# Splitting every weight tile by halves, with 32 bytes of space behind the rings

## The chip, the cores and the metric

One core of a Trainium2 chip runs the whole program in one launch. The metric is the time of that launch on the device in microseconds (us), the median of several runs. TensorE, VectorE (DVE), ScalarE (ACT), GpSimd (POOL) and SyncE (SP) each work through a list of instructions of their own in order and meet at semaphores.

## The reference

A trunk of two layers works on 256 tokens of width 1024, in f32. Each layer is a token mixer followed by product-key expert retrieval; the changed code feeds the weights to both.

```
for l in range(2):
    h = rms_norm(x) * (1 + sc1) + sh1
    x = x + g1 * mixer(h @ w_in) @ w_out
    h = rms_norm(x) * (1 + sc2) + sh2
    x = x + g2 * peer_ffn(h)

def peer_ffn(h):
    q = h @ wq
    sc = q . keys                       # 8 heads x 2 halves x 128 keys
    top 16 of each half, then top 16 of the 256 sums -> 16 experts a head, softmax gate
    act = gelu(h . u_tab[expert])
    return sum(gate * act * v_tab[expert])
```

## The kernel before

The experts are not gathered. The kernel computes all 16384 of them: 128 columns of the table `u` (128 experts each) give activations, which are multiplied by gates that are zero for the experts not chosen, and 128 rows of `v` bring the result back. So each layer streams 300 weight tiles of 128 x 1024 f32 (512 KB) from memory: 20 of `w_in`, 8 of `w_out`, 16 of `wq`, 128 of `u` (the stage "up", two halves of 64), 128 of `v` (the stage "down").

TensorE multiplies in a rounded f32 format, so each tile is split into `hi` (the rounded value) and `lo` (the rest), and each product is three matmuls: hi x hi, hi x lo, lo x hi (L361 to L363 for an up column, 24 matmuls of 256 columns; L927 for a down row, 12 of 512). The class `Stream` does this. `load` brings a tile into one of 4 `raw` buffers (SP issues the DMA). `split_halves` makes `hi` and `lo` in rings of 3 tiles. So the split of tile n needs the ring's place that tile n-3 leaves, and the load of tile n+4 the `raw` buffer that tile n leaves. There are three ways to make `lo`, and `kind` deals the tiles out to them by the shares in the table `SHARE` (by layer and stage: first half of up, second half, first half of down, second half) and `MIXSHARE`:

- "dve": ScalarE copies `raw` to `hi` (L201), VectorE subtracts, `lo = raw - hi` (L203);
- "pool": the same with the subtraction on POOL (L203 too);
- "dma": ScalarE writes `lo = -raw` rounded (L196), a DMA issued by POOL adds `raw` to it in memory (L197), ScalarE writes `hi` (L198).

A "dma" tile is split in two halves of 512 columns, k = 0 and 1; the others are split as a whole. `ahead`, called after each product, splits as far as `AHEAD = 2` tiles past the one now used (and a first half more, if that tile is "dma").

Beside the weights runs background work, fed in by `Background`: generators that emit a few VectorE instructions at a time with a charge in us, as long as the charged VectorE time is no more than 2 us ahead of the modelled TensorE time (2.6 us a column). `LOCOST` is what a "dve" `lo` is charged. In the first half of up it is the top-16 search (L787 to L838) and, in layer 0, modulation vectors (L285); in the second half and in down it is the gates (L865 to L886). The build's scheduler then orders each engine's list by when operands are expected and by program order.

Of the kernel before, what the change touches and what calls it, by code (L numbers as in the profile page):

```python
# [10 lines left out]
F32 = mybir.dt.float32  # L11
# [7 lines left out]
P = 128  # L19
D = 1024  # L20
# [16 lines left out]
MIXSTEP = 3.4  # L37
RANKS = (3, 2, 4, 1)
MODCOST = 1.2
LOCOST = 1.1  # L40
HALF = D // 2
MIXSHARE = {"dma": 0.4}
CONVCOST = 0.45
# [3 lines left out]
KTAKE = 3  # L47
CONVRANK = 2.5
PACE = (1.0, 2.6)
SHARE = (({"pool": 0.8}, {"dma": 0.25}, {"dma": 0.2}, {}),  # L50
         ({"pool": 0.7, "dma": 0.3}, {"dma": 0.25}, {"dma": 0.2}, {"dma": 0.1}))
NCOL = 94
NROW = 64 + 256 + 256 + 128
# [7 lines left out]
class Carve:  # L61


    def __init__(self, *tiles):
        self.tiles = tiles
        self.reset()
# [77 lines left out]
class Stream:  # L144
# [10 lines left out]
    def __init__(self, nc, pool, aps, bg):  # L155
        self.nc, self.pool, self.aps, self.bg = nc, pool, aps, bg
        self.nd = self.ns = 0
        self.raw = {}
        self.hi, self.lo = [pool.tile([P, self.RING, D], F32R, name=name) for name in ("hi", "lo")]
        self.depth = self.RAW  # L160
        self.share = {}
        self.acc = {"dma": 0.0, "pool": 0.0}
        self.by, self.kinds = "dve", {}
# [20 lines left out]
    def split_halves(self, upto):  # L184

        nc = self.nc
        while self.ns <= min(upto, 2 * len(self.aps) - 1):
            n, k = divmod(self.ns, 2)
            by = self.kind(n)
            if by != "dma" and upto < 2 * n + 1:  # L190
                return
            self.load(n)
            cols = slice(HALF * k, HALF * k + HALF) if by == "dma" else slice(0, D)
            raw, hi, lo = self.raw[n][:, cols], self.hi[:, n % self.RING, cols], self.lo[:, n % self.RING, cols]
            if by == "dma":
                nc.scalar.activation(out=lo, in_=raw, func=AF.Copy, scale=-1.0)  # L196
                nc.gpsimd.dma_start(out=lo, in_=raw, accum_op=ALU.add)  # L197
                nc.scalar.activation(out=hi, in_=raw, func=AF.Copy)  # L198
                self.ns += 1
            else:  # L200
                nc.scalar.activation(out=hi, in_=raw, func=AF.Copy)  # L201
                eng = nc.gpsimd if by == "pool" else nc.vector
                eng.tensor_tensor(out=lo, in0=raw, in1=hi.bitcast(F32), op=ALU.subtract)  # L203
                if by == "dve":
                    self.bg.charge(LOCOST)
                self.ns += 2
            if self.ns % 2 == 0:
                del self.raw[n]
                self.load(n + self.depth)
# [9 lines left out]
class Trunk:  # L219
# [35 lines left out]
        return self.stream.get(n)  # L255

    def ahead(self):
        self.stream.split_halves(2 * (self.pos + self.stream.AHEAD))

    def col(self, l, off, n):  # L260
        return self.cols[:, l * NCOL + off:l * NCOL + off + n]
# [676 lines left out]
    def experts(self, l, area):  # L938
# [13 lines left out]
        acts = [self.big(32, T) for _ in range(2)]  # L952
        self.stream.share = SHARE[l][0]
        run = self.up(hb, acts)
        next(run)
        self.stream.share = SHARE[l][1]
        acts += [self.big(32, T) for _ in range(2)]
# [5 lines left out]
        for i in range(2):  # L963
            self.bg.add(self.gates(1, acts[2:4], i, kept))
        self.stream.share = SHARE[l][2]
        run = self.down(acts)
        next(run)
        self.stream.share = SHARE[l][3]
        self.m = Carve(self.big(), self.big())
# [213 lines left out]
```

## Time and profile before

| what | value |
|---|---|
| median of 3 runs | 2092.47 us (2085.89 to 2093.71) |
| the profiled execution, its own time | 2067.38 us |
| its span, first to last instruction | 2065.3 us |
| TensorE busy | 1909.7 us, 92% of the span |
| mean granted TensorE clock | 0.968 |

A row of the profile's page or of the trace names a line of the kernel (L203), an engine, what is written and read (`lo<-raw,hi`), how often, and times. PE is TensorE and PEld its loading of weights. "Idle before" is time in which the engine did nothing ahead of the instruction, with what released it. The profiled execution is one run; its time is 1.2% under the median.

### The profile page before, as it was taken

The numbers are of one execution on the slowest core, as the hardware profiler recorded it, in microseconds if no ns is written. First come the engines' busy times: TensorE is split into PE (matmuls) and PEld (weight loads), VectorE is DVE, ScalarE is ACT, GpSimd is POOL, SyncE is SP. The second block draws the span as 40 slices with busy tenths as digits, with TensorE's granted clock in tenths as the row PEclk, the third lists the DMA queues.
The fourth block names the chain that finished last, engine by engine and source line by source line (L and its number), as shares of the span: only waits on it lengthen the run. The fifth ranks groups of instructions, "written<-read, shape, count | busy, mean of one in ns | idle before, by whom it ended". The sixth has DMA issues, their size and how long they took to land.

```text
span 2065.3 us, 36257 instructions
## 1 busy us (share of the span) xinstructions
PE 1909.7 (92%) x13718; PEld 1703.1 (82%) x13718; DVE 1417.3 (69%) x2949; ACT 1085.2 (53%) x1790; POOL 472.3 (23%) x361
## 2 busy tenths in 40 slices
PE   6897887999999999899998999888999999999998
PEld 4786887999999776678887899888999987777776
DVE  7887799467765877687568679904467668755554
ACT  4665533544455544545567665555554555555554
POOL 0112355651111111100011225766311111110001
PEclk7888998999999999999999999999999999999999
DMA  8987745757778888887657678777878888876673
GB/s 288 282 256 221 219 166 182 253 189 230 245 245 242 261 271 298 277 321 251 188 160 193 181 194 216 202 208 223 233 246 248 250 244 263 240 209 211 204 205 111
DMA packets 156945, 471.32 MB, mean 228 GB/s; under 512 B 17724, under 2 KB 19041, under 8 KB 156514
## 3 DMA queue, kind: packets, MB, share of 16 engines
q1 hardware_dynamic: 122786, 407.13, 57.6%
q0 software_dynamic: 33984, 61.88, 17.0%
q8 instruction: 107, 1.75, 0.3%
q14 instruction: 68, 0.56, 0.1%
HBM read 388.72 MB, written 18.36 MB: 197 GB/s over the span
## 4 chain that ended last, share of the span: by engine, by line
PE 49%; DMA 25%; DVE 12%; issue 7%; ACT 4%; POOL 2%; SPq 0%; POOLq 0%; DVEq 0%; ACTq 0%
PE acc L927 24%; DMA lo<-raw 17%; PE bank L363 7%; PE bank L361 7%; PE bank L362 7%; DMA raw<-v 3%; DMA raw<-u 2%; DVE lo L203 2%; DVE big L285 2%; DMA big<-wmod 1%; ACT hi L201 1%; POOL lo L197 1%; PE bank L878 1%; PE acc L878 1%; DVE big L817 1%
## 5 line engine op out<-in xcount | busy, mean ns | idle before, releaser
L363 PE MATMUL bank<-mid,lo 128*128 128x256 f32 x2432 | 699.5, 288 | 69.1 <-DMA lo<-raw 43.6
L201 ACT ACTIVATE hi<-raw 128x1024 fp32r<-128x1024 f32 x482 | 512.0, 1062 | 451.5 <-issue 193.3
L361 PE MATMUL bank<-mid,hi 128*128 128x256 f32 x2432 | 700.6, 289 | 5.5 <-ACT mid L1066 5.0
L362 PE MATMUL bank<-mid,hi 128*128 128x256 f32 x2432 | 692.9, 285 | 1.1 <-DVE mid L1069 1.1
L203 DVE TENSOR_TENSOR lo<-raw,hi 128x1024 fp32r<-128x1024 f32 x387 | 479.9, 1240 | 222.2 <-ACT hi L201 220.1
L927 PE MATMUL acc<-hi,mid 128*128 128x512 f32 x2048 | 579.1, 400 | 0.7 <-ACT mid L912 0.6
L363 PEld LDWEIGHTS bank<-mid,lo 128*128 128x128 f32 x2432 | 468.1, 193 | 82.1 <-DMA lo<-raw 54.9
L197 POOL DMA_DIRECT2D lo<-raw x236 | 204.7, 870 | 1204.9 <-ACT lo L196 894.4
L361 PEld LDWEIGHTS bank<-mid,hi 128*128 128x128 f32 x2432 | 467.7, 193 | 9.8 <-ACT mid L1066 7.4
L362 PEld LDWEIGHTS bank<-mid,hi 128*128 128x128 f32 x2432 | 468.1, 193 | 3.3 <-DVE mid L1069 2.6
L927 PEld LDWEIGHTS acc<-hi,mid 128*128 128x128 f32 x2048 | 383.6, 189 | 90.1 <-ACT mid L912 1.0
L927 PE MATMUL acc<-lo,mid 128*128 128x512 f32 x1024 | 330.2, 400 | 22.8 <-DMA lo<-raw 22.6
L203 POOL TENSOR_TENSOR lo<-raw,hi 128x1024 fp32r<-128x1024 f32 x95 | 243.3, 2567 | 124.5 <-ACT hi L201 124.5
L912 ACT ACTIVATE mid<-big 128x256 fp32r<-128x256 f32 x256 | 106.3, 416 | 304.3 <-PE acc L927 298.7
L927 PEld LDWEIGHTS acc<-lo,mid 128*128 128x128 f32 x1024 | 193.4, 189 | 79.2 <-DMA lo<-raw 32.8
L913 DVE TENSOR_TENSOR mid<-big,mid 128x256 fp32r<-128x256 f32 x256 | 108.1, 424 | 145.1 <-PE acc L927 105.5
L198 ACT ACTIVATE hi<-raw 128x512 fp32r<-128x512 f32 x236 | 147.6, 626 | 92.1 <-PE bank L362 42.9
L196 ACT ACTIVATE lo<-raw 128x512 fp32r<-128x512 f32 x236 | 147.0, 623 | 45.0 <-PE acc L927 43.6
L285 DVE SCALAR_TENSOR_TENSOR big<-big 128x1025 f32<-128x1025 f32 x96 | 129.1, 1352 | 42.9 <-DMA big<-wmod 42.5
L886 DVE SCALAR_TENSOR_TENSOR big<-acc,big 128x256 f32<-128x256 f32 x128 | 49.2, 418 | 80.3 <-PE acc L878 80.3
L873 DVE TENSOR_TENSOR og<-o,gidx 128x512 f16<-128x512 f16 x256 | 100.7, 434 | 1.1 <-PE bank L878 0.6
L897 ACT ACTIVATE big<-bank 128x256 f32<-128x256 f32 x256 | 93.6, 366 | 0.0
(200 smaller groups left out, 1583.1 us busy)
## 6 DMA issues: line engine op xcount, KB each, us to landing
raw<-u SPq DMA_DIRECT2D x256, 512.0 KB, 4.7
raw<-v SPq DMA_DIRECT2D x256, 512.0 KB, 4.1
lo<-raw POOLq DMA_DIRECT2D x236, 256.0 KB, 5.6
big<-wmod SPq DMA_DIRECT2D x96, 512.5 KB, 5.9
raw<-win SPq DMA_DIRECT2D x40, 512.0 KB, 5.3
raw<-wq SPq DMA_DIRECT2D x32, 512.0 KB, 4.6
kept<-o SPq DMA_DIRECT2D x64, 256.0 KB, 5.7
o<-kept SPq DMA_DIRECT2D x64, 256.0 KB, 4.6
```

The lines of the kernel that those rows point to most:

```text
L196: nc.scalar.activation(out=lo, in_=raw, func=AF.Copy, scale=-1.0)
L197: nc.gpsimd.dma_start(out=lo, in_=raw, accum_op=ALU.add)
L198: nc.scalar.activation(out=hi, in_=raw, func=AF.Copy)
L201: nc.scalar.activation(out=hi, in_=raw, func=AF.Copy)
L203: eng.tensor_tensor(out=lo, in0=raw, in1=hi.bitcast(F32), op=ALU.subtract)
L285: nc.vector.scalar_tensor_tensor(out=w, in0=w, scalar=1.0, in1=sc, op0=ALU.mult, op1=ALU.mult, accum_out=self.modT[:, l, j:j + 1])
L361: mm(out, whi, hhi, start=start, stop=False)
L362: mm(out, whi, hlo, start=False, stop=False)
L363: mm(out, wlo, hhi, start=False, stop=stop)
L912: nc.scalar.activation(out=a[:, 0], in_=src, func=AF.Copy)
L913: nc.vector.tensor_tensor(out=a[:, 1], in0=src, in1=a[:, 0].bitcast(F32), op=ALU.subtract)
L927: nc.tensor.matmul(self.acc[2 * tt + d], a[:, s, P * tt:P * tt + P], w[:, 512 * d:512 * d + 512], start=i == 0 and s == 0 and w is whi, st ...
```

## The change

`split_halves` treats every tile as it treated the "dma" tiles: in two halves of 512 columns, so that ScalarE, VectorE and POOL get two instructions of half the width. `ahead` asks for two whole tiles past the present one. `LOCOST` is now charged per half, and the "pool" share of layer 0's first half of up is 0.6. An unused tile `pad` of 8 f32 words lies behind the two rings, so all later tiles start 32 bytes higher.

```
@@ -37,7 +37,7 @@
 MIXSTEP = 3.4
 RANKS = (3, 2, 4, 1)
 MODCOST = 1.2
-LOCOST = 1.1
+LOCOST = 0.6
 HALF = D // 2
 MIXSHARE = {"dma": 0.4}
 CONVCOST = 0.45
@@ -47,7 +47,7 @@
 KTAKE = 3
 CONVRANK = 2.5
 PACE = (1.0, 2.6)
-SHARE = (({"pool": 0.8}, {"dma": 0.25}, {"dma": 0.2}, {}),
+SHARE = (({"pool": 0.6}, {"dma": 0.25}, {"dma": 0.2}, {}),
          ({"pool": 0.7, "dma": 0.3}, {"dma": 0.25}, {"dma": 0.2}, {"dma": 0.1}))
 NCOL = 94
 NROW = 64 + 256 + 256 + 128
@@ -157,6 +157,7 @@
         self.nd = self.ns = 0
         self.raw = {}
         self.hi, self.lo = [pool.tile([P, self.RING, D], F32R, name=name) for name in ("hi", "lo")]
+        pool.tile([P, 8], F32, name="pad")
         self.depth = self.RAW
         self.share = {}
         self.acc = {"dma": 0.0, "pool": 0.0}
@@ -187,23 +188,20 @@
         while self.ns <= min(upto, 2 * len(self.aps) - 1):
             n, k = divmod(self.ns, 2)
             by = self.kind(n)
-            if by != "dma" and upto < 2 * n + 1:
-                return
             self.load(n)
-            cols = slice(HALF * k, HALF * k + HALF) if by == "dma" else slice(0, D)
+            cols = slice(HALF * k, HALF * k + HALF)
             raw, hi, lo = self.raw[n][:, cols], self.hi[:, n % self.RING, cols], self.lo[:, n % self.RING, cols]
             if by == "dma":
                 nc.scalar.activation(out=lo, in_=raw, func=AF.Copy, scale=-1.0)
                 nc.gpsimd.dma_start(out=lo, in_=raw, accum_op=ALU.add)
                 nc.scalar.activation(out=hi, in_=raw, func=AF.Copy)
-                self.ns += 1
             else:
                 nc.scalar.activation(out=hi, in_=raw, func=AF.Copy)
                 eng = nc.gpsimd if by == "pool" else nc.vector
                 eng.tensor_tensor(out=lo, in0=raw, in1=hi.bitcast(F32), op=ALU.subtract)
                 if by == "dve":
                     self.bg.charge(LOCOST)
-                self.ns += 2
+            self.ns += 1
             if self.ns % 2 == 0:
                 del self.raw[n]
                 self.load(n + self.depth)
@@ -255,7 +253,7 @@
         return self.stream.get(n)
 
     def ahead(self):
-        self.stream.split_halves(2 * (self.pos + self.stream.AHEAD))
+        self.stream.split_halves(2 * (self.pos + self.stream.AHEAD) - 1)
 
     def col(self, l, off, n):
         return self.cols[:, l * NCOL + off:l * NCOL + off + n]
```

Two places show how the instructions move. The first is ScalarE's list in the second half of up in layer 0, around one "dma" tile and the "dve" tile behind it. L897 is the gelu that empties a column's PSUM bank (L895 after the change, where all lines from `split_halves` on stand two lower). Before:

```order
L198 ACTIVATE hi<-raw 128x512
L196 ACTIVATE lo<-raw 128x512
L198 ACTIVATE hi<-raw 128x512
L897 ACTIVATE big<-bank 128x256
L196 ACTIVATE lo<-raw 128x512
L201 ACTIVATE hi<-raw 128x1024
```

After:

```order
L197 ACTIVATE hi<-raw 128x512
L195 ACTIVATE lo<-raw 128x512
L197 ACTIVATE hi<-raw 128x512
L895 ACTIVATE big<-bank 128x256
L195 ACTIVATE lo<-raw 128x512
L199 ACTIVATE hi<-raw 128x512 x2
```

The "dma" tile's five rows stand as they stood, and the "dve" tile's one `hi` of 1024 columns has become two of 512.

The second place is VectorE's list in the first half of up in layer 0, where the top-16 search (L785 to L798) stands around the `lo` of a "dve" tile. Before:

```order
L787 MAX big<-big 128x8
L203 TENSOR_TENSOR lo<-raw,hi 128x1024
L791 MAX_INDEX big<-big 128x8
L788 MAX_INDEX big<-big 128x8
L798 TENSOR_TENSOR big<-big 128x256
```

After:

```order
L201 TENSOR_TENSOR lo<-raw,hi 128x512
L787 MATCH_REPLACE big<-big 128x256
L785 MAX big<-big 128x8
L788 MAX big<-big 128x8
L201 TENSOR_TENSOR lo<-raw,hi 128x512
L789 MAX_INDEX big<-big 128x8
```

The one `lo` has become two, and three instructions of the search now stand between them.

## Rows read from the trace of the kernel before

**Rows 1.** Windows: stretch, length, busy us (instructions) by engine, PEclk, DMA share, GB/s

```profile
255.00:275.00 20.00, 20.00 (x171) 20.00 (x170) 20.00 (x89) 9.40 (x15) 13.31 (x6) 1.00 0.58 184
...
335.00:355.00 20.00, 17.51 (x133) 17.09 (x132) 20.00 (x14) 7.36 (x11) 14.93 (x5) 0.91 0.72 256
...
375.00:395.00 20.00, 20.00 (x171) 20.00 (x170) 8.70 (x13) 12.13 (x17) 15.69 (x7) 1.00 0.75 246
```

The engines in it are PE, PEld, DVE, ACT, POOL, in this order.

**Rows 2.** Waits of TensorE, whole run: waiting line <- releaser: us, times, longest

```profile
PE bank L363 <- DMA lo<-raw: 43.6, 37, 2.8
PE bank L363 <- DVE lo L203: 24.7, 8, 7.3
PE acc L927 <- DMA lo<-raw: 22.6, 21, 3.1
```

**Rows 3.** Waits of TensorE from 235 to 453 us

```profile
PE bank L363 <- DVE lo L203: 23.2, 6, 7.3
PE bank L363 <- DMA lo<-raw: 1.7, 1, 1.7
```

**Rows 4.** Windows: the first half of up in layer 0

```profile
235.00:453.00 218.00, 193.03 (x1552) 191.37 (x1551) 174.11 (x397) 90.53 (x135) 133.24 (x52) 0.95 0.60 201
```

**Rows 5.** Windows: around the longest wait of that stage

```profile
312.00:319.00 7.00, 0.15 (x2) 0.00 (x0) 7.00 (x5) 1.33 (x2) 5.93 (x2) 0.72 0.02 5
319.00:325.00 6.00, 5.50 (x26) 5.50 (x26) 6.00 (x9) 0.62 (x1) 0.00 (x0) 0.50 0.70 261
```

**Rows 6.** Lines of VectorE, 235 to 453 us: count | busy us, mean ns | idle before

```profile
L285 DVE SCALAR_TENSOR_TENSOR big<-big 128x1025 f32<-128x1025 f32 x16 | 31.8, 2018 | 10.2 <-DMA big<-wmod 10.1
L203 DVE TENSOR_TENSOR lo<-raw,hi 128x1024 fp32r<-128x1024 f32 x13 | 22.9, 1759 | 8.6 <-ACT hi L201 8.6
...
L817 DVE TENSOR_TENSOR big<-big 128x2048 f32<-128x2048 f32 x4 | 13.3, 3320 | 0.0
```

**Rows 7.** Single lines, whole run: count: ns min/median/max, first and last start

```profile
L203 DVE TENSOR_TENSOR lo<-raw,hi x387: 1160/1225/3393, 19.9 to 2042.6; 128x1024 fp32r<-128x1024 f32 x194
L203 POOL TENSOR_TENSOR lo<-raw,hi x95: 2342/2398/4474, 242.5 to 1458.7; 128x1024 fp32r<-128x1024 f32 x95
L817 DVE TENSOR_TENSOR big<-big x8: 2268/2285/4455, 311.4 to 1418.0; 128x2048 f32<-128x2048 f32 x8
L331 POOL TENSOR_TENSOR big<-big x12: 726/758/2188, 169.8 to 1194.0; 128x256 f32<-128x256 f32 x12
L913 DVE TENSOR_TENSOR mid<-big,mid x256: 413/425/427, 661.8 to 2038.8; 128x256 fp32r<-128x256 f32 x128
L285 DVE SCALAR_TENSOR_TENSOR big<-big x96: 1161/1220/3446, 8.6 to 946.3; 128x1025 f32<-128x1025 f32 x96
```

**Rows 8.** Timeline of VectorE in that wait: start us, us, what

```profile
311.45 4.28 DVE L817 TENSOR_TENSOR big<-big 128x2048 f32<-128x2048 f32 x1
...
318.24 1.21 DVE L203 TENSOR_TENSOR lo<-raw,hi 128x1024 fp32r<-128x1024 f32 x1
```

**Rows 9.** The page's groups: ScalarE's two widths of `hi`

```profile
L201 ACT ACTIVATE hi<-raw 128x1024 fp32r<-128x1024 f32 x482 | 512.0, 1062 | 451.5 <-issue 193.3
...
L198 ACT ACTIVATE hi<-raw 128x512 fp32r<-128x512 f32 x236 | 147.6, 626 | 92.1 <-PE bank L362 42.9
```

**Rows 10.** The page's busy us by engine, share of the span, instructions

```profile
PE 1909.7 (92%) x13718; PEld 1703.1 (82%) x13718; DVE 1417.3 (69%) x2949; ACT 1085.2 (53%) x1790; POOL 472.3 (23%) x361
```

**Rows 11.** Timeline of ScalarE, the two halves of one "dma" tile (layer 1, up)

```profile
1274.28 0.64 ACT L198 ACTIVATE hi<-raw 128x512 fp32r<-128x512 f32 x1 [0.19 <-ACT big L897]
...
1275.72 0.64 ACT L198 ACTIVATE hi<-raw 128x512 fp32r<-128x512 f32 x1 [0.28 <-PE bank L362]
```

**Rows 12.** The page's DMA queues: packets, MB, share of 16 engines

```profile
q1 hardware_dynamic: 122786, 407.13, 57.6%
q0 software_dynamic: 33984, 61.88, 17.0%
```

More of the change, by code (lines that the diff above doesn't have):

```diff
@@ L39 @@
 MODCOST = 1.2
-LOCOST = 1.1
+LOCOST = 0.6
 HALF = D // 2
@@ L49 @@
 PACE = (1.0, 2.6)
-SHARE = (({"pool": 0.8}, {"dma": 0.25}, {"dma": 0.2}, {}),
+SHARE = (({"pool": 0.6}, {"dma": 0.25}, {"dma": 0.2}, {}),
          ({"pool": 0.7, "dma": 0.3}, {"dma": 0.25}, {"dma": 0.2}, {"dma": 0.1}))
@@ L159, in __init__ @@
         self.hi, self.lo = [pool.tile([P, self.RING, D], F32R, name=name) for name in ("hi", "lo")]
+        pool.tile([P, 8], F32, name="pad")
         self.depth = self.RAW
@@ L189, in split_halves @@
             by = self.kind(n)
-            if by != "dma" and upto < 2 * n + 1:
-                return
             self.load(n)
-            cols = slice(HALF * k, HALF * k + HALF) if by == "dma" else slice(0, D)
+            cols = slice(HALF * k, HALF * k + HALF)
             raw, hi, lo = self.raw[n][:, cols], self.hi[:, n % self.RING, cols], self.lo[:, n % self.RING, cols]
@@ L198, in split_halves @@
                 nc.scalar.activation(out=hi, in_=raw, func=AF.Copy)
-                self.ns += 1
             else:
@@ L205, in split_halves @@
                     self.bg.charge(LOCOST)
-                self.ns += 2
+            self.ns += 1
             if self.ns % 2 == 0:
@@ L257, in ahead @@
     def ahead(self):
-        self.stream.split_halves(2 * (self.pos + self.stream.AHEAD))
+        self.stream.split_halves(2 * (self.pos + self.stream.AHEAD) - 1)
     def col(self, l, off, n):
```

## The prediction

> **What bounds the kernel now.** I went from the busy shares to the stages, from there to the waits of TensorE, and then into the one stage whose wait the change can touch.
>
> TensorE is the bound: in the stretch from 375 to 395 us it is busy for all 20.00 us, with 171 matmuls [rows 1]. A column of the up stage has 24 of them, so a column that waits for nothing takes 20.00 / 171 x 24 = 2.81 us. What a change can win is TensorE's waiting. The waits of TensorE over the whole run have three large entries [rows 2]: 43.6 and 22.6 us for the `lo` of a "dma" tile, and 24.7 us for the `lo` of a "dve" tile. The first two make 66.2 us. The third is almost all in one stage: of the 24.7 us, 23.2 us in 6 waits, the longest 7.3 us, lie between 235 and 453 us [rows 3]. That is the first half of up in layer 0, where the top-16 search runs on VectorE in the background. The reader is to see that `lo` of a "pool" tile is in no list: those tiles are never late.
>
> In that stage 64 columns take 218.0 us [rows 4]; 64 x 2.81 = 180, so 38 us are lost, more than the 25 us or so of waits. The rest is the clock. One stall shows it: from 312 to 319 us TensorE is busy 0.15 us, and from 319 to 325 us, with a granted clock of 0.50 (1.2 of its 2.4 GHz), it does 26 matmuls in 5.50 us [rows 5]; at 20.00 / 171 each they would take 3.0 us.
>
> Why is `lo` late? VectorE is full: 20.00 of 20 us in each of the five stretches from 255 to 355 us (the first and the last stand in [rows 1]). And its instructions are longer there than elsewhere. `lo` on VectorE takes 1759 ns on average in this stage, L817 3320, L285 2018 [rows 6]; their medians over the run are 1225, 2285 and 1220 [rows 7]. In the stall above L817 takes 4.28 us, and `lo` stands behind it [rows 8]. They lengthen where POOL is at work: in this stage it is busy 133.24 of the 218 us [rows 4], with `lo` instructions of 2398 ns [rows 7].
>
> **The change, part by part.**
>
> *Halves on VectorE, POOL and ScalarE.* No row shows VectorE or POOL with 512 f32 columns and two inputs. The bounds are 256 and 1024 columns: 425 and 1225 ns on VectorE (L913, L203), 758 and 2398 on POOL (L331, L203) [rows 7]. A line through each pair gives 425 + 256 x 800 / 768 = 692 and 758 + 256 x 1640 / 768 = 1305 ns, and I take these. A pair is 1.38 and 2.61 us, 0.16 and 0.21 more than now (0.85 to 2.45 us and 1.5 to 4.8 us from the ends). ScalarE has the row: 626 ns against 1062 [rows 9], +0.19 us a tile. Over the run: 482 tiles x 0.19 = 92 us more of ScalarE, 387 x 0.16 = 62 us more of VectorE. ScalarE is busy 53% of the span, VectorE 69% [rows 10], beside a TensorE that is nearly always at work: nearly all is hidden. It is not hidden where the mixers' chains run through ScalarE; 55 non-"dma" tiles lie there (counted in the built programs), 55 x 0.19 = 10 us, of which I put 2 us on the path. If that cover were gone, 10.
>
> *More lead.* Now a "dve" tile n is split after column n-3 has ended: `hi` 1.06, then `lo` 1.23, ready 2.29 us after that end. With halves the first `hi` waits for the first half of column n-3 alone. The trace shows this for "dma" tiles, which are in halves already: the second half's L198 starts 1.44 us after the first, released by TensorE [rows 11]. So the first half would be ready half a column (1.4) earlier plus 2.29 - (0.63 + 0.69) = 0.97 us: 2.4 us earlier; the second half is needed 1.4 us later than the first and gains as much. This is won once per run of stalls: VectorE never empties between 255 and 355 us, so what the first stall saves the next ones have already used. I count it twice, for that run and for waits outside it.
>
> *Shares 0.8 to 0.6, LOCOST 1.1 to 0.6.* In the built programs the stage goes from 48 "pool", 14 "dve" and 2 "dma" tiles to 37, 26 and 1. VectorE gets 26 x 1.38 = 36.0 for 14 x 1.23 = 17.2 us: +19. Against it the planner charges 2 x 0.6 on 2 of 5 columns in place of 1.1 on 1 of 5, 0.48 for 0.22 of a step of 2.6, so it queues (2.6 - 0.48) / (2.6 - 0.22) = 0.89 as much background per column. Real `lo` work per column grows by 0.4 x 1.38 - 0.2 x 1.23 = 0.31 us, and 0.26 us of charged background makes room: VectorE's queue per column stays as long as it is.
>
> *What POOL does to VectorE.* The stretching of the three groups in [rows 6] is 13 x 0.53 + 4 x 1.04 + 16 x 0.80 = 24 us. With 37 tiles of 2.61 for 48 of 2.40 us POOL's share of the stage falls to 0.84 of what it is, and a wait for one POOL instruction can last 1.3 in place of 2.4 us, 0.54: together 0.45 per VectorE instruction. The two other groups go from 17 to 7.6 us; `lo` is 52 instructions then, at 0.53 x 0.45 = 0.24: 12.5 for 7. So 24 becomes 20 in these three. I take 8 us on the path, 4 for these and as much again for the groups outside [rows 6]; the ends are 4 and, were the 24 us gone altogether, 24.
>
> The Trainium skill ("SBUF — State Buffer", Who interferes with whom) says that a VectorE instruction with two SBUF inputs and a POOL instruction that reads SBUF lock each other out, for the whole instruction. The 4.28 us of L817 agree. By it POOL's halves also wait for VectorE twice per tile; what that would do is the second rival.
>
> *"dma" tiles.* They are 118 before and after, with the same instructions; in the built order ScalarE does their halves at the same places. The 66.2 us stay. One of the two at the head of the search stage becomes "dve", and its wait of 1.7 us [rows 3] goes.
>
> *The gap.* In the built layout `hi` and `lo` stay, and `raw`, `big` and `mid` move from 32 bytes past a multiple of 64 onto one. On the engines this costs and gives nothing: L285 works wholly in `big`, at 1220 ns for 1025 columns; L203 reads `raw` but also `hi`, which lies on such a multiple already, at 1225 for 1024 [rows 7]. For DMA, the accumulating queue took 17.0% of 2065.3 us for 236 transfers, 1.49 us each; the plain queue took 57.6% for 407.13 MB, 0.77 us for as much [rows 12]. At best the gap brings 0.72 us to each of the 58 waits of [rows 2], 42 us. A loss is excluded: the target `lo` already lies as `raw` will. I take 0, since an accumulate reads two operands, and 2 x 0.77 = 1.53 explains the 1.49.
>
> The Trainium skill ("DMA: Bandwidth & Descriptors", How a descriptor splits into AXI transactions) counts in pieces of 256 bytes. `raw` starts 96 bytes past such a boundary now and 128 then, so by it nothing is gained; no run here shows it yet.
>
> *Sum.* 8 (stretching) + 2 x 2.4 (lead) + 1.7 (the "dma" tile) + 3 (clock: of the 13 us lost there that are no wait, as stalls shorten) - 2 (ScalarE) = 15 us. The profiled execution took 2067.38 us, 1.2% less than the median of the runs; 2052 for it, and 2092.47 - 15 = **2077 us** against that median.
>
> **The rivals.**
>
> *Nothing moves.* VectorE stays full, its 12 further tiles eat what POOL lets go, and the stalls stay where they are. For it: the +19 us of `lo` work in the stage, and halves that the built order puts next to each other late in the stage. Against it: the lead, which is in the order. 2082 to 2103 us, around 2090.
>
> *Slower: POOL and VectorE lock each other twice as often.* The place is the same stage. If the stretch per VectorE instruction does not fall with POOL's shorter ones, 52 halves at 0.53 add 28 in place of 7 us, and the halves' own overhead 26 x 0.16 = 4; less the lead, 21 + 4 - 5 = 20: 2112 us. It decides if a half `lo` on VectorE takes over 1.1 us on average there. Against it: 1305 ns is the most that one POOL half can hold.
>
> *The gap speeds the accumulate.* Up to 42 us on top: 2035 to 2070. For it: the accumulate runs at half the plain rate. Against it: it reads twice as much.
>
> **How the numbers follow.** A measurement here tells 0.5% (10 us) from no change. My case 0.45, of which 0.05 falls short of 10 us; nothing moves 0.30; slower 0.13; the gap 0.12. Faster 0.53, same 0.34, slower 0.13. The range takes in my case, the second and half of the last: 2050 to 2100. My case alone is 2064 to 2086.
>
> **What would show it.** TensorE's waits for `lo` from VectorE fall from 23.2 to about 10 us in that stage, and the stage from 218 to 203; L817's mean falls below 2.9 us; a half `lo` takes about 0.69 us outside the stage, 0.95 in it; POOL's about 1.3. Waits for "dma" tiles stay near 66 us. I am wrong if those waits fall by over 15 us, if TensorE newly waits for `lo` from POOL, or if the stage does not get shorter.

## The result

The changed kernel takes 2027.99 us (median of 4 runs, 2021.12 to 2037.85) against 2089.94 us (4 runs) of the kernel before: a ratio of 0.9707, with a 95% interval of 0.9652 to 0.9763. On a second chip it gave 0.9747 (0.9718 to 0.9776). It is faster, as forecast, by 62 us on the first chip and 53 on the second in place of 15; 2028 lies below the range of 2050 to 2100.

**The profile after.** The profiled execution took 2021.12 us (span 2019.4 us), 46 us less than the one of before; the medians differ by 62. In the changed kernel the lines of `split_halves` and all behind them stand two lower. First the page's busy times by engine and its DMA queues, to be held against [rows 10] and [rows 12]:

```profile
PE 1891.7 (94%) x13718; PEld 1711.1 (85%) x13718; DVE 1472.8 (73%) x3360; ACT 1130.2 (56%) x2272; POOL 483.7 (24%) x432
...
q1 hardware_dynamic: 122786, 407.13, 58.7%
q0 software_dynamic: 33984, 61.88, 17.4%
```

The reader is to see that TensorE does its 13718 matmuls in 18 us less of busy time. Its instructions are the same, so its clock or its pace changed. Its idle time fell by 28 us, from 155.6 (2065.3 less 1909.7) to 127.7. VectorE and ScalarE are busier by 55.5 and 45.0 us. The accumulating queue takes 0.174 x 2019.4 / 236 = 1.49 us per transfer, as before.

The waits of TensorE, whole run [rows 2] (waiting line, releaser: us, times, longest):

```profile
PE bank L361 <- DMA lo<-raw: 27.1, 18, 6.1
PE acc L925 <- DMA lo<-raw: 22.3, 18, 4.6
PE bank L361 <- DVE lo L201: 16.5, 15, 3.5
```

and those from 229 to 441 us alone, the first half of up in layer 0 [rows 3]:

```profile
PE bank L361 <- DVE lo L201: 15.7, 13, 3.5
```

The first line (L363 before, L361 after) makes the products of the mixers as well as those of up. Its wait for "dma" tiles fell from 43.6 us in 37 waits to 27.1 in 18. Taken apart by stage, it fell in the four halves of up from 31.3 to 14.0 us and stayed outside them (12.3 before, 13.1 after). The wait for VectorE in the search stage fell from 23.2 to 15.7. Down's wait for "dma" tiles did not move.

TensorE's own pace, in stretches in which it waits for nothing. The windows hold 15 columns and 63 rows of before, then 20 columns and 63 rows of after (columns: stretch, length, busy us and instructions of PE, PEld, DVE, ACT, POOL, clock, DMA share, GB/s):

```profile
363.80:406.40 42.60, 42.60 (x362) 42.60 (x361) 18.06 (x21) 22.97 (x33) 29.68 (x12) 1.00 0.74 253
887.89:1064.29 176.40, 176.40 (x757) 141.68 (x756) 121.07 (x165) 93.66 (x126) 0.00 (x0) 1.00 0.72 240
```

```profile
1232.06:1289.65 57.59, 57.59 (x482) 57.59 (x481) 57.59 (x231) 38.20 (x73) 44.58 (x39) 1.00 0.84 237
874.91:1046.32 171.41, 171.41 (x757) 141.89 (x756) 123.27 (x226) 92.50 (x189) 0.00 (x0) 1.00 0.72 248
```

At a granted clock of 1.00 in all four, a column takes 42.60 / 15 = 2.84 us before and 57.59 / 20 = 2.88 after; a row takes 176.40 / 63 = 2.80 before and 171.41 / 63 = 2.72 after. TensorE waits for nothing in these windows, so its matmuls themselves got shorter in down and longer in up. (The 2.81 us of the prediction, from 171 matmuls that touch a window of 20 us, is a little low.)

With that the big stages can be taken apart: length from the first matmul to the last, less 64 columns or rows at the stage's own pace, leaves what is lost to waits, to a lower clock and to the gates' matmuls (15 to 16 us in the second half of up and again in the first half of down, before and after).

| stage of 64 tiles | before: length, lost | after: length, lost |
|---|---|---|
| layer 0, up, first half | 217.8, 36.0 | 211.3, 27.0 |
| layer 0, up, second half | 208.2, 26.4 | 204.4, 20.1 |
| layer 0, down, first half | 226.3, 47.1 | 229.8, 55.7 |
| layer 0, down, second half | 179.4, 0.2 | 174.3, 0.2 |
| layer 1, up, first half | 209.6, 27.8 | 202.2, 17.9 |
| layer 1, up, second half | 208.6, 26.8 | 202.6, 18.3 |
| layer 1, down, first half | 201.2, 22.0 | 193.9, 19.8 |
| layer 1, down, second half | 182.3, 3.1 | 176.5, 2.4 |
| sum | 1633.4, 189.4 | 1595.0, 161.4 |

By this account 28 of the 38 us that these stages got shorter are lost time that went: 34 us less in up, 6 more in down, where the first half in layer 0 got longer (why is open). The other 10 are pace: 256 rows x 0.08 = 20 us won, 256 columns x 0.04 = 10 lost. The account takes pace and waits as if they added up; the run with a gap of 64 bytes below shows that in up they do not. The remaining 8 of the 46 us lie outside these stages.

### The profile page after: what moved, and what is told of

Same layout as the page of the kernel before. It is cut to its first block, busy times and chain, and to the rows that moved or that the text cites. A ratio compares the mean times of both kernels' runs of the same rounds, so it can differ in the third digit from the quotient of the medians.

```text
span 2019.4 us, 37831 instructions
## 1 busy us (share of the span) xinstructions
PE 1891.7 (94%) x13718; PEld 1711.1 (85%) x13718; DVE 1472.8 (73%) x3360; ACT 1130.2 (56%) x2272; POOL 483.7 (24%) x432
## 4 chain that ended last, share of the span: by engine, by line
PE 63%; DMA 15%; DVE 11%; issue 6%; ACT 2%; POOL 2%; SPq 0%; POOLq 0%; DVEq 0%; ACTq 0%
PE acc L925 27%; PE bank L361 11%; PE bank L359 11%; PE bank L360 10%; DMA lo<-raw 10%; DMA big<-wmod 2%; DVE lo L201 2%; DMA raw<-v 2%; DVE big L283 2%; PE acc L876 1%; PE bank L876 1%; POOL lo L196 1%; DVE big L786 1%; POOL lo L201 1%; DVE big L787 1%
## 5 line engine op out<-in xcount | busy, mean ns | idle before, releaser
L199 ACT ACTIVATE hi<-raw 128x512 fp32r<-128x512 f32 x964 | 577.4, 624 | 366.3 <-PE bank L360 236.6
L361 PE MATMUL bank<-mid,lo 128*128 128x256 f32 x2432 | 700.2, 288 | 43.8 <-DMA lo<-raw 27.1
L201 DVE TENSOR_TENSOR lo<-raw,hi 128x512 fp32r<-128x512 f32 x798 | 550.3, 714 | 212.5 <-ACT hi L199 207.6
L925 PE MATMUL acc<-hi,mid 128*128 128x512 f32 x2048 | 570.3, 396 | 0.1
L361 PEld LDWEIGHTS bank<-mid,lo 128*128 128x128 f32 x2432 | 474.4, 195 | 51.9 <-DMA lo<-raw 31.6
L359 PEld LDWEIGHTS bank<-mid,hi 128*128 128x128 f32 x2432 | 473.4, 195 | 10.3 <-ACT mid L1064 7.0
L360 PEld LDWEIGHTS bank<-mid,hi 128*128 128x128 f32 x2432 | 474.2, 195 | 2.4 <-DVE mid L1067 2.0
L925 PE MATMUL acc<-lo,mid 128*128 128x512 f32 x1024 | 326.0, 397 | 22.4 <-DMA lo<-raw 22.3
L201 POOL TENSOR_TENSOR lo<-raw,hi 128x512 fp32r<-128x512 f32 x166 | 261.8, 1652 | 97.5 <-ACT hi L199 88.7
L197 ACT ACTIVATE hi<-raw 128x512 fp32r<-128x512 f32 x236 | 147.5, 625 | 86.7 <-PE bank L360 54.9
L283 DVE SCALAR_TENSOR_TENSOR big<-big 128x1025 f32<-128x1025 f32 x96 | 122.3, 1281 | 35.0 <-DMA big<-wmod 26.8
L871 DVE TENSOR_TENSOR og<-o,gidx 128x512 f16<-128x512 f16 x256 | 96.5, 418 | 0.8 <-PE bank L876 0.4
L895 ACT ACTIVATE big<-bank 128x256 f32<-128x256 f32 x256 | 93.7, 366 | 0.0
L876 PEld LDWEIGHTS <-o 128*128 128x128 f16 x2048 | 67.3, 97 | 15.9 <-issue 13.1
```

Of the source, the lines that this page charges most:

```text
L283: nc.vector.scalar_tensor_tensor(out=w, in0=w, scalar=1.0, in1=sc, op0=ALU.mult, op1=ALU.mult, accum_out=self.modT[:, l, j:j + 1])
L359: mm(out, whi, hhi, start=start, stop=False)
L360: mm(out, whi, hlo, start=False, stop=False)
L361: mm(out, wlo, hhi, start=False, stop=stop)
L876: nc.tensor.matmul(b[:, 64 * j:64 * j + 64], o1[:, j // 2, :, j % 2], og[:, j // 2, s, :, j % 2], start=s == 0, stop=s == 1)
L925: nc.tensor.matmul(self.acc[2 * tt + d], a[:, s, P * tt:P * tt + P], w[:, 512 * d:512 * d + 512], start=i == 0 and s == 0 and w is whi, st ...
```

## The experiments

Two causes are to be told apart, each with rivals: the gap (TensorE's pace) and the halves (the lost time). Each run was timed in 5 rounds beside the kernel before on its chip; the first four ran on one chip, the next four on a second, the last four on a third.

| run | median us | of before | interval |
|---|---|---|---|
| gap alone | 2075.50 | 0.9970 | 0.9946 to 0.9993 |
| change without the gap | 2039.45 | 0.9792 | 0.9764 to 0.9820 |
| change, gap of 64 bytes | 2042.38 | 0.9822 | 0.9792 to 0.9852 |
| change, shares as before | 2033.70 | 0.9773 | 0.9743 to 0.9803 |
| the change again | 2033.53 | 0.9747 | 0.9718 to 0.9776 |
| change, gap just ahead of mid | 2032.38 | 0.9762 | 0.9735 to 0.9790 |
| change, mid's place by stage | 2035.15 | 0.9759 | 0.9732 to 0.9787 |
| change, `lo` in one piece | 2065.32 | 0.9916 | 0.9888 to 0.9945 |
| change, bound of `ahead` as before | 2045.20 | 0.9814 | 0.9780 to 0.9848 |
| change, mid as one tile, placed by stage | 2026.16 | 0.9727 | 0.9695 to 0.9758 |
| the same, rings shifted in down | 2040.13 | 0.9793 | 0.9760 to 0.9825 |
| mid as one tile, `lo` used later | 2007.66 | 0.9634 | 0.9596 to 0.9673 |

**Gap alone.** In the kernel before:

```
         self.hi, self.lo = [pool.tile([P, self.RING, D], F32R, name=name) for name in ("hi", "lo")]
+        pool.tile([P, 8], F32, name="pad")
```

> The kernel before with the 32-byte pad behind the rings and nothing else. Theory A (the layout sets TensorE's own pace: in the changed kernel's profile a down row that waits for nothing took 2.72 in place of 2.80 us and an up column 2.88 in place of 2.84): the pace moves here too, the second half of down in layer 0 goes from 179.4 to about 174.5 us, down gains about 256 x 0.08 = 20 us and up loses about 256 x 0.04 = 10, so about 10 us faster, 2080. Theory B (the pace is set by the halves, the pad does nothing): 2090, the stage stays at 179. Theory C (the pad is what brought most of the 61 us): about 2030.

The ratio is 0.9970, by which the gap alone is worth about 6 us (1.5 to 11 by the interval). Here are a window of 37 rows of down and, ahead of it, one of 14 columns of up:

```profile
372.15:412.47 40.32, 40.32 (x338) 40.32 (x337) 15.03 (x21) 21.62 (x31) 27.25 (x12) 1.00 0.69 228
976.50:1077.14 100.64, 100.64 (x445) 83.33 (x444) 60.63 (x73) 53.66 (x72) 0.00 (x0) 1.00 0.65 201
```

40.32 / 14 = 2.88 and 100.64 / 37 = 2.72 us: the gap alone makes the new pace, in whole tiles too. Theory A holds; C, that it brought most of the gain, falls.

**The change without the gap.** The `pad` line is left out.

> The changed kernel without the pad. Theory A (the layout sets TensorE's pace, the halves do the rest): a wait-free down row is back at 2.80 us and an up column at 2.84, so about 10 us slower than the changed kernel, 2038, or about 52 faster than the kernel before. Theory B (halves set the pace): 2028, and rows stay at 2.72 us. Theory C (the pad brought most): 2075 to 2090.

The ratio is 0.9792, which is 0.0045 or 9 us above the change's 0.9747, measured on another chip; the intervals overlap. A row is back at 2.80 us (63 rows):

```profile
880.30:1056.75 176.45, 176.45 (x757) 141.74 (x756) 124.01 (x226) 92.75 (x189) 0.00 (x0) 1.00 0.72 241
```

So the change without its gap (halves, shares and the bound of `ahead` together) gives some 43 us, most of the gain. Its paces are those of before, so the stages can be compared as they are: the four halves of up take 821.4 us against 844.2, those of down 790.6 against 789.2. The gain between the profiles lies in up.

**A gap of 64 bytes.** `pool.tile([P, 16], F32, name="pad")`.

> The changed kernel with a pad of 64 in place of 32 bytes, so that the buffers behind the rings again start 32 bytes past a multiple of 64. Theory A in the form that the place within 64 bytes counts: as without the pad, down rows at 2.80 and up columns at 2.84 us, about 2038. In the form that any shift away from the old places counts: as the changed kernel, rows at 2.72, 2028.

```profile
1266.11:1291.31 25.20, 25.20 (x218) 25.20 (x217) 25.20 (x103) 16.86 (x33) 20.66 (x19) 1.00 0.91 247
870.35:1046.74 176.39, 176.39 (x757) 142.03 (x756) 123.40 (x226) 92.38 (x189) 0.00 (x0) 1.00 0.71 241
```

63 rows in 176.39 us, 2.80 each, and 9 columns in 25.20 us, also 2.80. Rows are as without a gap, so the place counts and not the shift. But columns came out at 2.80, faster than both 2.84 and 2.88, which neither form had foreseen. In the built layout `mid` starts 96 bytes past a multiple of 128 without a gap, 0 past it with 32 and 32 past it with 64: places within 128 bytes, not 64, have to be told apart.

The time is 0.9822, not told apart from the 0.9792 without a gap, though columns faster by 0.04 us should have won 256 x 0.04 = 10 us. The four halves of up take 819.9 us here with columns at 2.80, 821.4 without a gap at 2.84, and 820.5 in the change at 2.88. So a faster column does not make a shorter stage of up here; a part of what it wins comes back as waiting (for `lo` 38.1 us in up, 35.5 without a gap).

**Shares as before.**

```
-LOCOST = 0.6
+LOCOST = 0.55
-SHARE = (({"pool": 0.6}, {"dma": 0.25}, {"dma": 0.2}, {}),
+SHARE = (({"pool": 0.8}, {"dma": 0.25}, {"dma": 0.2}, {}),
```

> The changed kernel, but with the planner's numbers as before: the pool share 0.8 in the first half of up in layer 0, and 0.55 charged per half (1.1 per tile). If the shares carry a part: that stage, 211.3 us after the change, goes back towards 217.8, and the time to about 2034. If only the halves count in it: no difference, 2028. If the further lo work on VectorE had cost: the stage below 211 and the time below 2025.

The ratio is 0.9773, and its interval overlaps that of the change: what the shares are worth in the whole isn't settled. In their stage TensorE's wait for `lo` from VectorE is 22.1 us in 9 waits, near the 23.2 of before, and the stage is 217.2 us long against 211.3 and, in the repeat of the change, 210.6. So some 6 us of that stage are the shares', and without them the rest of the change leaves it where it was (217.8 us before).

**The change again**, as a base.

> The changed kernel once more, beside the runs below on one chip, as their base. The runs so far gave ratios to the kernel before of 0.9707 (the change), 0.979 (without the gap), 0.997 (the gap alone). If halves and gap simply add: 0.979 x 0.997 = 0.976. If the gap is worth more behind halves: 0.971.

The ratio is 0.9747, nearer to the plain sum of the two parts (0.976, within its interval) than to 0.971.

**The gap ahead of mid.** The `pad` line moves from behind the rings to the place where `mid` is first made, so that `raw` and `big` stay where they were before.

> The changed kernel with the 32 bytes moved from behind the rings to just ahead of mid: raw and big start where they did before the change, mid and what follows where they do after it. If the place of mid, TensorE's own operand, sets the pace: rows of down 2.72 us and columns of up 2.88 us as in the changed kernel, and the same time. If it is raw or big (what the other engines and the DMAs write and read at the same time): 2.80 and 2.84, and the time of the kernel without a gap, 0.979 of before.

A window of 22 columns and one of 63 rows:

```profile
1257.42:1320.78 63.36, 63.36 (x530) 63.36 (x529) 63.36 (x208) 40.65 (x79) 53.55 (x45) 1.00 0.82 234
874.39:1045.81 171.42, 171.42 (x758) 141.89 (x756) 123.05 (x226) 92.79 (x190) 0.00 (x0) 1.00 0.73 248
```

Rows take 2.72 us and columns 2.88, and the time is that of the change. So the pace does not come from the place of `raw` and `big`, which other engines and the DMAs use. That it comes from `mid`, TensorE's own operand, and not from what lies behind it, is borne out by the later runs, in which a stage reads at another place in `mid`.

**Mid's place by stage.** No gap; `mid` gets 16 words more, up reads it from word 0, down from word 8.

```
-        return self.one.tile([P, *shape], dt, name="mid", tag="mid", bufs=2)
+        t = self.one.tile([P, 2064], dt, name="mid", tag="mid", bufs=2)[:, skip:skip + 2048]
...
-        ab = self.mid(4, 2, T, dt=F32R)
+        ab = self.mid(4, 2, T, dt=F32R, skip=8)
```

> The changed kernel without the gap, but mid gets a place by stage: up reads it 32 bytes past a multiple of 64 (as before the change), down reads it 32 bytes further, on a multiple of 64 (0 past a multiple of 128 in layer 0, 64 past it in layer 1). If mid's place sets the pace, and does so in opposite senses where it is the moving operand (up) and the stationary one (down): columns at 2.80 to 2.84 us and rows at 2.72, about 256 x 0.06 = 15 us faster than the changed kernel, 0.968 to 0.970 of before. If 64 is another case than 0, rows of layer 1 stay at 2.80. If raw or big set it: rows at 2.80 everywhere, 0.979.

Windows of columns and rows of layer 0, then of layer 1:

```profile
233.73:262.18 28.45, 28.45 (x242) 28.45 (x241) 28.45 (x122) 16.62 (x31) 18.79 (x13) 1.00 0.68 228
945.74:1043.66 97.92, 97.92 (x434) 81.08 (x432) 62.06 (x109) 51.92 (x107) 0.00 (x0) 1.00 0.65 202
1263.11:1314.95 51.84, 51.84 (x434) 51.84 (x433) 51.84 (x174) 32.92 (x64) 44.51 (x37) 1.00 0.79 221
1929.19:2016.04 86.85, 86.85 (x374) 69.86 (x373) 47.28 (x83) 46.50 (x95) 5.15 (x6) 1.00 0.64 192
```

Rows take 97.92 / 36 = 2.72 us in layer 0 (`mid` 0 past a multiple of 128) and 86.85 / 31 = 2.80 in layer 1 (64 past it). So 64 is not 0. Columns, whose two parts of `mid` lie at 32 and 96 in one layer and the other way round in the other, take 28.45 / 10 = 2.85 and 51.84 / 18 = 2.88 us. That is slower than with both parts at 32 (2.80) or both at 96 (2.84), so the place of each operand by itself does not give the pace; how the two act together is open. The hoped 15 us did not come: 0.9759 beside the change's 0.9747.

**`lo` in one piece.** `hi` still in halves:

```
                 nc.scalar.activation(out=hi, in_=raw, func=AF.Copy)
-                eng = nc.gpsimd if by == "pool" else nc.vector
-                eng.tensor_tensor(out=lo, in0=raw, in1=hi.bitcast(F32), op=ALU.subtract)
-                if by == "dve":
-                    self.bg.charge(LOCOST)
+                if k:
+                    raw, hi, lo = self.raw[n], self.hi[:, n % self.RING], self.lo[:, n % self.RING]
+                    eng = nc.gpsimd if by == "pool" else nc.vector
+                    eng.tensor_tensor(out=lo, in0=raw, in1=hi.bitcast(F32), op=ALU.subtract)
+                    if by == "dve":
+                        self.bg.charge(2 * LOCOST)
```

> The changed kernel with hi still written in halves by ScalarE, but lo subtracted in one piece of 1024 columns again on VectorE or POOL. Theory D (what halves win at the dma tiles is that a raw buffer is freed and the next load issued earlier, so that fewer load bytes share the DMA engines with the accumulate: from before to after its issue-to-landing fell from 6.1 to 5.6 us in the second half of up in layer 0 and from 5.1 to 4.5 in the first half of down in layer 1): raw comes free about 0.5 us later than in the changed kernel, the accumulate's time goes about half the way back, to 5.9 and 4.8 us, and the whole is 10 to 20 us slower than the changed kernel. Theory E (hi in halves alone does it, ScalarE being blocked for less time): same as the changed kernel. The 23.2 us wait for lo from VectorE in the top-16 stage should come back in part in both.

The ratio is 0.9916, which is 0.0169 above the change on the same chip: 35 us (33 between the profiles of this run and of the repeat of the change). This is the largest part that was found, and more than theory D had set. D's own signs came only in part: the accumulate took 5.0 us in the first half of down in layer 1, as far back as D had said or further, but 5.6 in the second half of up in layer 0, where it did not go back at all.

D's shape is seen best in the first half of up in layer 1, where all but a few tiles are "pool" or "dma". What SP's queue waits for there before it can issue a load, of before, of the change and of this run (releaser: us, times, longest):

```profile
SPq L168 <- DMA lo<-raw: 152.3, 20, 9.5
SPq L168 <- POOL lo L203: 24.6, 16, 3.7
```

```profile
SPq L169 <- POOL lo L201: 109.0, 34, 6.0
SPq L169 <- DMA lo<-raw: 42.7, 17, 7.3
```

```profile
SPq L169 <- DMA lo<-raw: 138.2, 18, 10.1
SPq L169 <- POOL lo L203: 32.6, 15, 5.0
```

and what the accumulates take there from issue to landing (median us, last number), in the same order:

```profile
lo<-raw POOLq DMA_DIRECT2D x38, 256.0 KB, 6.8
```

```profile
lo<-raw POOLq DMA_DIRECT2D x38, 256.0 KB, 5.5
```

```profile
lo<-raw POOLq DMA_DIRECT2D x38, 256.0 KB, 6.7
```

SP issues the loads in order, and the load that follows a "dma" tile into its `raw` buffer has to wait until the accumulate has landed. Before, SP stood in this wait for 152.3 of 210 us, and the loads behind it left together: three at 1284.59, 1285.02 and 1285.49 us, beside accumulates issued at 1286.12 and 1287.83 us. With `lo` in halves it stands there for 42.7 us; it waits for POOL instead, and more loads leave one by one (1280.59, 1282.25, 1283.28 us): 11 loads of that stage follow the one ahead within 0.6 us, for 25 before and 26 with `lo` whole. While one accumulate of that stage is under way, 0.99 MB of loads move beside it on average before, 0.76 in the change and 1.00 with `lo` whole (DMA packets between its issue and its landing, 36 accumulates). TensorE's wait for "dma" tiles there is 20.3 us before, 12.3 in the change and 23.0 here.

All these numbers come back when `lo` alone is made whole, and the "dma" tiles' own instructions are the same in all three kernels. The other runs bear it out: SP's wait for accumulates there is 149.5 us with the gap alone and 41.3 in the change without the gap. An accumulate that stands longer in POOL's own list is not the cause, since POOL issues it 0.30 us (median) after ScalarE's `lo` in all three. Theory E falls as the account of the whole. Whether loads that leave one by one make the accumulates land earlier, or the other way round, was not tried apart; each helps the other.

This stage is a smaller part of the 33 us than it looks: it takes 209.6 us before, 202.2 in the change and 216.4 here, but 207.4 in the repeat of the change, which leaves 9 us. The search stage has 14 (224.6 us against 210.6, with 26.6 us of waits for `lo` from VectorE; 26 tiles are "dve" there, 14 before). Some 7 lie outside the eight stages, and the rest is spread; no run takes these apart.

The Trainium skill ("DMA: Bandwidth & Descriptors", Issuing engines are not separate DMA queues) says that transfers issued by different engines run on the same 16 DMA engines and interleave. The traces of this stage fit that: the accumulates issued by POOL take 6.8 us with 0.99 MB of SP's loads beside them and 5.5 with 0.76.

**Bound of `ahead` as before.**

```
-        self.stream.split_halves(2 * (self.pos + self.stream.AHEAD) - 1)
+        self.stream.split_halves(2 * (self.pos + self.stream.AHEAD))
```

> The changed kernel with the bound of ahead as it was: one half tile further ahead. If how far ahead the splits are asked for carries part of the gain (the further half would make ScalarE wait for a ring place that TensorE has not left, as before the change): slower by 5 to 10 us than the change's 0.9747 to before, 0.978 to 0.980. If the build's scheduler sets the order anyway: 0.9747.

The ratio is 0.9814, which is 0.0067 or 14 us above the change, on another chip; the intervals do not overlap. So the bound carries a part that I had not priced at all. That it does so by a wait for ring places, the reason given, is not shown: the first half of up in layer 1 is shorter than in the change (195.7 us). The first half of down takes 233.8 us in layer 0 and 199.9 in layer 1 (229.8 and 193.9 in the change), and the wait at a norm's first product is longer:

```profile
PE bank L359 <- ACT big L323: 16.7, 1, 16.7
```

against 10.3 us in the change and 11.2 in its repeat. Of the 14 us between the profiles of this run and of the repeat, 10 lie outside the eight stages. The bound also moves a tile from one kind to another at the stages' edges, so these parts aren't separated.

**Mid as one tile, placed by stage.** With the gap, `mid` is one tile of 4104 words on a multiple of 128; up reads its two parts from word 8 and word 2056, down from word 0.

> The changed kernel with mid as one tile whose base is a multiple of 128 bytes: up reads both parts 32 bytes past it, down reads on it. The paces seen so far: columns 2.80 us with both parts at 32 past a multiple of 128 (pad of 64), 2.84 at 96, 2.88 at 0; rows 2.72 at 0, 2.80 at 32, 64 and 96. If the place within 128 bytes sets the pace, each stage by itself: columns 2.80 and rows 2.72, 256 x 0.08 = 20 us faster than the changed kernel, 0.965 of before. If what is won goes into waits for lo, which is not ready earlier: half of it, 0.970.

A window of 15 columns and one of 36 rows:

```profile
1245.95:1287.95 42.00, 42.00 (x362) 42.00 (x361) 42.00 (x171) 27.66 (x54) 35.16 (x31) 1.00 0.89 247
943.23:1041.15 97.92, 97.92 (x434) 81.11 (x433) 62.03 (x108) 51.95 (x107) 0.00 (x0) 1.00 0.65 202
```

Columns take 2.80 us and rows 2.72, as expected of both. The time is 0.9727, 2 thousandths below the change on another chip, with intervals that overlap. The four halves of up take 815.5 us together, against 820.5 and 826.2 in the two profiles of the change: 5 to 11 us of the 20. Waits for `lo` took back a part of the rest: in up those for "dma" tiles are 19.3 us, against 14.0 and 16.2 in the two profiles of the change.

**Rings shifted in down.** On top of that, `hi` and `lo` become one tile, and tiles of down lie 8 words further in it.

```
+    def place(self, n, part):
+        at = (part * self.RING + n % self.RING) * D + (8 if n % 300 >= 172 else 0)
+        return self.rings[:, at:at + D]
```

> The kernel of the run before with the rings as one tile, so that tiles of down lie 32 bytes past a multiple of 128 in hi and lo as well (in up they stay on it). If TensorE's moving operand has its good place at 32 in down as in up (where it took 3.5 ns off a matmul): rows fall from 2.72 to about 2.68 us, 256 x 0.04 = 10 us faster, 0.960. If only the stationary operand counts in down, or the two have to differ in a certain way: rows stay at 2.72 or go back towards 2.80, 0.965 to 0.975.

The second reading holds: the ratio is 0.9793, and rows are back at 2.79 us:

```profile
900.00:1000.00 100.00, 100.00 (x430) 80.31 (x430) 73.28 (x139) 53.92 (x109) 0.00 (x0) 1.00 0.75 252
```

(100.00 / 430 x 12). The run is 14 us slower than the one it builds on.

**`lo` used later.** On top of mid as one tile, TensorE's order:

```
...
+            for h in (0, 4):
+                for c in range(h, h + 4):
+                    cs = slice(P * c, P * c + P)
+                    mm(b, whi[:, cs], hhi[:, c], start=c == 0, stop=False)
+                    mm(b, whi[:, cs], hlo[:, c], start=False, stop=False)
+                for c in range(h, h + 4):
+                    mm(b, wlo[:, P * c:P * c + P], hhi[:, c], start=False, stop=c == NC - 1)
...
+                order = [(tt, s, w, d) for d in range(2) for s, w in ((0, whi), (1, whi), (0, wlo)) for tt in range(2)]
```

> The kernel with mid placed by stage (two runs before this one), and TensorE's own order changed so that lo is needed later and halves are left earlier: in a column the 8 products with hi of four chunks, then their 4 with lo; in a row all six matmul pairs of the first half of the columns, then those of the second, with lo last in each. If TensorE's remaining waits are lateness of lo, as the chain says (27 us in up and 22 in down for dma tiles, 17 for dve tiles in the changed kernel, 49 waits in all), a half is needed 0.7 us later in each and raw comes free up to 1.3 us earlier in down: 20 to 40 us faster than the run it builds on, 0.945 to 0.955 of before. If the loads are the bound in those stages: no faster, 0.965.

The time is 2007.66 us, less than that of both kernels, and 18 us less than the run it builds on (6 between their profiles): just short of the 20 to 40. The ratio of 0.9634 is nearer to the 0.965 that was set for loads as the bound than to 0.945 to 0.955, so the run does not decide between the two. Its waits for "dma" tiles are

```profile
PE bank L381 <- DMA lo<-raw: 26.2, 22, 6.9
...
PE acc L942 <- DMA lo<-raw: 18.2, 10, 4.2
```

which is 26.2 and 18.2 us for 31.9 and 23.7, and the first half of down in layer 0 takes 217.7 us for 228.5. TensorE's wait for `lo` from VectorE rose from 18.9 to 20.6 us, and the second half of up in layer 0 got no shorter (205.4 for 201.9). So lateness of `lo` is part of what bounds these stages, and not all.

## Why the prediction was wrong

The sign was right, the size was a quarter. In its own terms, the prediction failed at two steps: it let the wait for "dma" tiles stand, and it let the gap do nothing to the engines. Undone one at a time, the parts of the change are worth about 35 us (`lo` in halves), 14 (the bound of `ahead`), 9 (the gap) and 5 (the shares), by the ratios above; they overlap, since together they give 53 on the second chip, and the 5 is within the noise. `hi` in halves was not undone by itself.

- *"Dma" tiles: "The 66.2 us stay."* This step failed. The waits fell to 27.1 + 22.3 = 49.4 us, by more than the 15 that were to show the prediction wrong. They make 17 of the 28 us by which TensorE's idle time fell; the wait for VectorE, on which most of the sum was built, makes 8. I had looked at the "dma" tiles' own instructions, which did not change, and not at the load that waits behind them in SP's queue.
- *More lead: "won once per run of stalls", counted twice, 4.8 us.* In the search stage, where it was counted, hardly any of it shows: with the shares as before, TensorE waits 22.1 us for VectorE there, for 23.2 before the change. What the halves bring lies elsewhere. In the first half of up in layer 1 a load leaves on average 14.3 and 14.5 us ahead of its column in the two profiles of the change, for 13.8 before and 14.0 with `lo` whole, so the `raw` buffers come free somewhat earlier, and fewer loads run beside an accumulate. With `lo` whole, this stage and the search stage have some 23 of the 33 us between the profiles.
- *The bound of `ahead`* had no term. It measured 14 us; how is open.
- *The gap: "On the engines this costs and gives nothing."* This failed in its premise. The rows I read [rows 7] were VectorE's, and TensorE, which reads `mid` in each of its matmuls there, was left out. The pace moved by -0.08 us a row and +0.04 a column, and the gap is worth 6 us alone and 9 behind the halves. The part on DMA held: 1.49 us per accumulate before and after, so the rival "the gap speeds the accumulate" falls; that the time came out nearest to its range is chance.
- *Halves' own cost.* 692 ns were estimated for VectorE and 626 for ScalarE; the medians over the run are 689 and 622. POOL's least is 1262, but its median 1483 and its mean 1652 where I had 1305. ScalarE got 45 us busier, VectorE 55, where 92 and 62 were said; TensorE's waits for ScalarE grew by 2.8 us at one product of the mixers and hardly elsewhere, near the 2 that were put on the path, so that nearly all is hidden was right.
- *Stretching: 24 to 20 us in three groups.* It did not fall. VectorE's rows of the search stage [rows 6]:

```profile
L201 DVE TENSOR_TENSOR lo<-raw,hi 128x512 fp32r<-128x512 f32 x54 | 55.7, 1049 | 15.2 <-ACT hi L199 15.2
L283 DVE SCALAR_TENSOR_TENSOR big<-big 128x1025 f32<-128x1025 f32 x16 | 24.9, 1581 | 3.4 <-DMA big<-wmod 3.3
...
L815 DVE TENSOR_TENSOR big<-big 128x2048 f32<-128x2048 f32 x4 | 12.1, 3024 | 0.0
```

  Against medians of 689, 1220 and 2285 ns that is 54 x 0.36 + 16 x 0.36 + 4 x 0.74 = 28 us. L815 stays above the 2.9 that was to show the step right. The modulation vectors gained, the more numerous `lo` halves lost. The step that failed is POOL's share, which was to fall to 0.84 of what it was. POOL's rows of that stage, before and after:

```profile
L203 POOL TENSOR_TENSOR lo<-raw,hi 128x1024 fp32r<-128x1024 f32 x50 | 132.3, 2652 | 84.2 <-ACT hi L201 84.1
```

```profile
L201 POOL TENSOR_TENSOR lo<-raw,hi 128x512 fp32r<-128x512 f32 x76 | 130.8, 1736 | 82.4 <-ACT hi L199 79.9 <-PE bank L361 1.0
```

  Fewer tiles keep POOL busy for as long, 130.8 for 132.3 us: a pair of halves takes 3.47 us there in place of the 2.61 that were set. POOL's halves are stretched too, as the second rival has it. A half `lo` of VectorE takes 1.05 us there, over the 0.95 of my case and not yet the 1.1 from which the slower rival was to decide.
- *The stage: 218 to 203, waits for VectorE 23.2 to 10.* They came to 211.3 and 15.7. With the shares as before they are 217.2 and 22.1, so nearly all of this hangs on the shares, which had no price of their own. They pay only behind the halves: with the new shares and `lo` whole the stage takes 224.6 us.

## What to carry to other kernels

A piece that ends earlier can be worth more than the wait it shortens: ask which buffer it frees, which load that releases, and what that load collides with. Look at the queue that issues the loads as one more engine with an order, and read what it waits for. When a layout moves, list every engine that reads the moved buffers, the bound one first, and compare its pace in windows without a wait. A faster pace is only won where the stage does not wait for something else.

## What was not expected of the hardware

In these kernels the time of a matmul depends on where its operands start within 128 bytes. The paces below are taken at a granted clock of 1.00, in windows without a wait. All slices inside the tiles start multiples of 512 bytes apart.

| matmuls | `mid` starts at (mod 128) | rings at | us | ns each |
|---|---|---|---|---|
| column, 24 of 256; `hi`/`lo` stationary, `mid` moving | 32 | 0 | 2.80 | 117 |
| | 96 | 0 | 2.84 | 118 |
| | 0 | 0 | 2.88 | 120 |
| | one part 32, the other 96 | 0 | 2.85, 2.88 | 119, 120 |
| row, 12 of 512; `mid` stationary, `hi`/`lo` moving | 0 | 0 | 2.72 | 227 |
| | 32, 64, 96 | 0 | 2.80 | 233 |
| | 0 | 32 | 2.79 | 233 |

The row with two places does not follow from those with one. Matmuls of the other stages were not looked at, and why it is so is not shown by any run. A gap of 32 bytes was worth 6 to 9 us here. By the paces down won 20 us and up lost 10; by the lengths of the stages, with halves, down takes 774.5 and 775.5 us in the change's two profiles for 790.6 without the gap, and up 820.5 and 826.2 for 821.4.
